# Gate and up of two feed forwards as seven block products instead of eight

## The chip, the cores and the metric

The kernel runs as one program on one core of one Trainium2 chip. The metric is device time in microseconds (us) of a whole run. The kernel before takes 2904.51 us, the median of three runs (2902.11 to 2906.32).

The engines' names in what follows are those of the profile: PE is TensorE (matmuls), PEld its weight load, DVE is VectorE, ACT is ScalarE, POOL is GpSimd, SP is SyncE, which issues most of the DMAs.

## The reference

The model is two transformer layers over 512 tokens and 256 context tokens, with 1024 features. A layer is: feed forward, attention, feed forward, each with an RMS norm, a learned shift and scale in front of it, and a gate on the result. What matters here, cut to the feed forwards:

```python
D_MODEL, SEQ, CTX_LEN, D_FF, DEPTH = 1024, 512, 256, 2816, 2

def _rmsnorm(x, w):
    y = x * lax.rsqrt(jnp.mean(x * x, axis=-1, keepdims=True) + EPS)
    return y * w

def _pre(h, gain, shift, scale):
    return _rmsnorm(h, gain) * (1.0 + scale) + shift

def _swiglu(h, w_gate, w_up, w_down):
    return (jax.nn.silu(h @ w_gate) * (h @ w_up)) @ w_down

for i in range(DEPTH):
    mx = (silu(c) @ ada_w[i] + ada_b[i]).reshape(B, 9, 1, D)      # the modulation, tokens
    mc = (silu(c_ctx) @ ada_w[i] + ada_b[i]).reshape(9, D)        # and context
    fx = _swiglu(_pre(hx, norm_w[i, 0], mx[:, 0], mx[:, 1]), ffn_w_gate[i, 0], ffn_w_up[i, 0], ffn_w_down[i, 0])
    hx = hx + 0.5 * mx[:, 2] * fx          # the same for hc with mc
    ...                                    # attention: i = 0 grouped, in windows; i = 1 differential
    fx = _swiglu(_pre(hx, norm_w[i, 2], mx[:, 6], mx[:, 7]), ffn_w_gate[i, 1], ffn_w_up[i, 1], ffn_w_down[i, 1])
    hx = hx + 0.5 * mx[:, 8] * fx          # the same for hc, but not in the last layer
return _rmsnorm(hx, final_norm_w)
```

All of it is in fp32. The four feed forwards are called first to fourth here: (layer 0, f 0), (0, 1), (1, 0), (1, 1). Attention stands between the first and the second and between the third and the fourth. The second and the third follow one another directly.

## The kernel before, in words

**Data.** Activations lie with features on the partitions: hT is [128, 8, 768], eight feature blocks, each with 256 context tokens and 512 tokens. An fp32 product is made from three matmuls in a faster format, which keeps only part of the mantissa: each operand is split into a high part (a cast) and a low part (what is left), and high x high, high x low and low x high are summed in PSUM. So every weight tile and every activation exists twice.

**Weights.** `weights` (its lines are 55 and 56 of the profile) reads 512 KB with a DMA that SP issues into w_raw (four buffers), ACT casts to w_hi (L55), and POOL subtracts to w_lo (L56); two buffers each.

**Input of a feed forward.** xh and xl, the scaled input in two parts, are made while the stage before writes its result: for each feature block d, as soon as the residual is in hT (`residual`, L311, DVE, reading PSUM), `x_block` squares it (ACT, L206), adds the squares into acc (POOL L208, the last block on DVE), and `x_parts` makes xh (ACT, L193) and xl (DVE, L194) for context and tokens. The normalization itself is linear, so its factor rstd is applied behind the projections. `norm` sums acc over partitions with a matmul against ones (PE, L239) and `rsqrt` makes rstd from it (ACT, and DVE L219 to L223).

**Blocks.** The 2816 hidden features are 22 blocks of 128. For a block, `project` (matmuls at L266) multiplies eight feature blocks x three parts x two column cuts of 384 tokens, for gate and again for up: 96 matmuls. Two extra columns carry the shift through the projection; they come out as the bias (DVE copy, L271). Then g = gate x rstd and u = up x rstd (DVE L304, PSUM input), silu on ACT, and the product (u + bias) x g in two parts, context and tokens (DVE, L961). ACT casts it to hh (L965), POOL subtracts to hl (L966).

**Down.** Blocks are taken in groups of 5, 5, 4, 4 and 4. A group's down projection (`gemm`, L68, L70, L72, per feature block d one PSUM tile with 256 and 512 columns) comes after the first block of the next group, the last group's at the end. There each d is followed by `x_block` of the next stage.

**Modulation.** The nine vectors of a layer are products of `ada_w` with two conditions. They are fill work: `ada_block` (L131) loads 512 KB and makes one or two products with a sum on DVE. 36 of these blocks fall into the second feed forward and 36 into the third.

**Order.** The engines' queues are in order. A scheduling pass of the framework decides, from the program's dependencies and a model of time, in which order each engine issues. Pools give buffers out again when their last reader is done. In PSUM, the feed forwards have four tiles "big" of two banks each.

## Time and profile before

| | |
|---|---|
| runs | 2904.51 us (2902.11 to 2906.32) |
| profiled execution | 2902.44 us, span 2900.6 us |
| mean granted clock of TensorE | 0.982 |
| PE busy | 2770.0 us, 95% of the span |
| DVE, POOL, ACT busy | 1555.9, 1311.2, 972.4 us |
| second feed forward | 986.8 to 1547.5 us |
| third feed forward | 1547.5 to about 2089 us |

How to read it: an engine's share of the span is an average over stages with different limits. PE's 95% says that it is the bound most of the time, not that the others have time at every place. In the rows that follow, a line is a group of instructions of one source line, engine and form, with its number, its mean duration and, in brackets, the idle time of its engine in front and what ended it. In views in order of time, the first number is the start in us from the beginning of the span, the second the duration. The stretches of a view of windows have, for every engine, the busy time and the number of instructions.

### The profile page before, as it was taken

Reading aid. Unit: us, or ns where it says so; the run is one execution under the profiler, and the core shown is the slowest. Engines: PE = TensorE matmul, PEld = TensorE weight load, DVE = VectorE, ACT = ScalarE, POOL = GpSimd, SP = SyncE. Lnnn points to the kernel's source line nnn. Section 1 sums busy time; section 2 is a strip of 40 time slices with the busy share of each in tenths; the row PEclk is TensorE's granted clock in tenths of the full one; section 3 lists DMA queues with packets and bytes.
Section 4 is the critical chain, followed back from the end, with each engine's and each line's share of the span. In section 5 each row is a group of like instructions: output and inputs, shape, how many; then the busy total and the mean of one; then the engine's idle time right before and its main releaser. Section 6 shows DMA issues by size and latency. Waiting matters only on the chain. (4 is left out here: it accounts for less than half of the span.)

```text
span 2900.6 us, 40961 instructions
## 1 busy us (share of the span) xinstructions
PE 2770.0 (95%) x16150; PEld 2593.4 (89%) x16150; DVE 1555.9 (54%) x2683; ACT 972.4 (34%) x1749; POOL 1311.2 (45%) x762
## 2 busy tenths in 40 slices
PE   5899999999989899999999999999989999999998
PEld 3899999989877799999998999999988887799998
DVE  7955555567887544444447333344467678522223
ACT  4322122145666421221224212221345555422223
POOL 4443343355443443333335433333465665555553
PEclk7999999999999999999999999999999999999999
DMA  6333333333242323233223232232232333233331
GB/s 240 121 112 108 125 105 118 124 115 100 82 144 81 99 78 112 76 106 117 74 90 106 75 118 84 91 120 88 85 98 74 90 89 114 83 92 100 102 105 44
DMA packets 113423, 296.38 MB, mean 102 GB/s; under 512 B 12880, under 2 KB 30928, under 8 KB 113232
## 3 DMA queue, kind: packets, MB, share of 16 engines
q1 hardware_dynamic: 112944, 293.66, 31.8%
q8 instruction: 128, 2.10, 0.3%
q14 instruction: 63, 0.52, 0.1%
q10 hardware_dynamic: 288, 0.10, 0.0%
HBM read 260.42 MB, written 15.20 MB: 95 GB/s over the span
## 5 line engine op out<-in xcount | busy, mean ns | idle before, releaser
L56 POOL TENSOR_TENSOR w_lo<-w_raw,w_hi 128x1024 fp32r<-128x1024 f32 (+2 forms) x377 | 802.1, 2128 | 1072.1 <-ACT w_hi L55 1055.6
L266 PE MATMUL big<-xh,w_hi 128*128 128x384 f32 (+3 forms) x2816 | 696.6, 328 | 38.7 <-DVE xh L831 19.5
L55 ACT CAST w_hi<-w_raw 128x1024 fp32r<-128x1024 f32 (+2 forms) x377 | 337.4, 895 | 1132.6 <-PE big L70 394.1
L266 PE MATMUL big<-xl,w_hi 128*128 128x384 f32 (+3 forms) x2816 | 693.6, 327 | 8.3 <-DVE xl L832 5.0
L266 PE MATMUL big<-xh,w_lo 128*128 128x384 f32 (+3 forms) x2816 | 693.6, 328 | 2.3 <-POOL w_lo L56 2.3
L266 PEld LDWEIGHTS big<-xh,w_hi 128*128 128x128 f32 x2816 | 502.5, 191 | 47.2 <-DVE xh L831 22.3
L266 PEld LDWEIGHTS big<-xl,w_hi 128*128 128x128 f32 x2816 | 500.3, 191 | 10.5 <-DVE xl L832 6.3
L266 PEld LDWEIGHTS big<-xh,w_lo 128*128 128x128 f32 x2816 | 497.8, 190 | 3.8 <-POOL w_lo L56 3.3
L131 DVE SCALAR_TENSOR_TENSOR ada_junk<-w_raw,s_bc 128x1024 f32<-128x1024 f32 x224 | 342.4, 1546 | 291.6 <-DMA w_raw<-ada_w 290.4
L271 DVE COPY bias<-big 128x2 f32<-128x2 f32 x176 | 27.7, 157 | 621.1 <-PE big L266 620.9
L68 PE MATMUL big<-hh,w_hi 128*128 128x512 f32 (+1 forms) x1200 | 327.6, 344 | 0.0
L70 PE MATMUL big<-hl,w_hi 128*128 128x512 f32 (+1 forms) x1200 | 327.3, 344 | 0.0
L72 PE MATMUL big<-hh,w_lo 128*128 128x512 f32 (+1 forms) x1200 | 326.8, 344 | 0.0
L311 DVE SCALAR_TENSOR_TENSOR hT<-big,mod,hT 128x512 f32<-128x512 f32 (+1 forms) x288 | 167.6, 618 | 176.7 <-PE big L72 176.4
L70 PEld LDWEIGHTS big<-hl,w_hi 128*128 128x128 f32 x1200 | 226.1, 188 | 29.5
L72 PEld LDWEIGHTS big<-hh,w_lo 128*128 128x128 f32 x1200 | 225.0, 188 | 28.6
L68 PEld LDWEIGHTS big<-hh,w_hi 128*128 128x128 f32 x1200 | 224.9, 188 | 27.2
L966 POOL TENSOR_TENSOR hl<-tb,hh 128x768 fp32r<-128x768 f32 (+1 forms) x88 | 152.3, 1730 | 183.2 <-ACT hh L965 181.9
L961 DVE SCALAR_TENSOR_TENSOR tb<-tb,bias,ta 128x512 f32<-128x512 f32 (+1 forms) x154 | 176.1, 1177 | 8.7 <-DVE tb L304 0.5
L285 PE MATMUL half<-xh,w_hi 128*128 128x384 f32 (+3 forms) x464 | 155.5, 335 | 20.6 <-DVE ta L297 18.8
L965 ACT CAST hh<-tb 128x768 fp32r<-128x768 f32 (+1 forms) x88 | 68.7, 781 | 276.5 <-DVE tb L961 276.5
L285 PE MATMUL half<-xl,w_hi 128*128 128x384 f32 (+3 forms) x464 | 153.8, 331 | 0.0
(215 smaller groups left out, 3677.6 us busy)
## 6 DMA issues: line engine op xcount, KB each, us to landing
w_raw<-ffn_gu SPq DMA_DIRECT2D x176, 512.0 KB, 3.3
w_raw<-ada_w SPq DMA_DIRECT2D x128, 512.0 KB, 3.3
w_raw<-ffn_d SPq DMA_DIRECT2D x96, 256.0 KB, 2.7
w_raw<-ffn_d SPq DMA_DIRECT2D x64, 320.0 KB, 2.9
w_raw<-diff_in SPq DMA_DIRECT2D x24, 512.0 KB, 3.2
ada_raw<-ada_w SPq DMA_DIRECT2D x16, 512.0 KB, 7.2
w_raw<-gqa_in SPq DMA_DIRECT2D x12, 512.0 KB, 3.5
og<-god SPq DMA_DIRECT2D x6, 768.0 KB, 6.5
```

The source lines that it names most:

```text
L55: nc.scalar.copy(out=hi[:, :cols], in_=raw[:, :cols])
L56: nc.gpsimd.tensor_tensor(out=lo[:, :cols], in0=raw[:, :cols], in1=hi[:, :cols].bitcast(F32), op=ALU.subtract)
L68: nc.tensor.matmul(o, wh, xh, start=(k == 0), stop=False)
L70: nc.tensor.matmul(o, wh, xl, start=False, stop=False)
L72: nc.tensor.matmul(o, wl, xh, start=False, stop=(k == n - 1))
L131: getattr(nc, engines[s]).scalar_tensor_tensor(out=junk, in0=raw, scalar=1.0, in1=self.sbc[:, s], op0=ALU.mult, op1=ALU.mult, accum_out=se ...
L266: mm(ps[:, c, :e - s], w[:, k], x[:, k, s:e], start=first, stop=last)
L285: mm(ps[:, :e - s], w_[:, k], x[:, k, s:e], start=(k == 0 and i == 0), stop=(k == ND - 1 and i == 2))
L311: self.nc.vector.scalar_tensor_tensor(out=h, in0=o, scalar=self.mv(l, s, c, d), in1=h, op0=ALU.mult, op1=ALU.add)
L961: nc.vector.scalar_tensor_tensor(out=u[:, tk], in0=u[:, tk], scalar=bu[:, s:s + 1], in1=g[:, tk], op0=ALU.add, op1=ALU.mult)
L965: nc.scalar.copy(out=hh[:, toks], in_=u[:, toks])
L966: nc.gpsimd.tensor_tensor(out=hl[:, toks], in0=u[:, toks], in1=hh[:, toks].bitcast(F32), op=ALU.subtract)
```

## The change

In the second and the third feed forward, a block's gate and up are one product of 2x2 blocks: the weight matrix has gate and up as its rows of blocks and the even and odd feature blocks as its columns; the input has the even and odd feature blocks as rows and the first and last 384 of the 768 tokens as columns. It is formed with seven products of blocks instead of eight, in the way of Strassen and Winograd: sums of weight blocks times sums of input blocks, added to the four results. A product is four pairs of feature blocks x three parts, 12 matmuls of 386 columns (384 and the two of the bias): 84 per block. The first and the fourth feed forward keep the old path.

With it comes:

- **Operands.** Instead of xh and xl there are seven operands for each pair of feature blocks, 28 slots in two tiles (opx, opy), each split into two parts. `operands`, called once per feature block where `x_block` was, makes them for every odd d: differences of scaled halves on DVE, casts on ACT, low parts on POOL or DVE.
- **Weight sums.** `up_open` loads the block's 2 x 512 KB and forms four sums of 512 columns (`total`, DVE); five halves of 512 and one of 1024 are split on ACT and POOL.
- **Results.** Products go to single PSUM banks (eight). Copies out of PSUM on ACT, additions from PSUM on DVE, and the scaling by rstd on DVE and POOL make g and u. Product 4 of a block, and with it all that follows (silu, product, hh, hl), is put into the next block (`up_end`).
- **Groups** of 4, 4, 4, 4, 3 and 3 blocks in these two stages; down projections with two feature blocks per weight load.
- **Buffers.** Weight tiles have one name and four buffers, in the new stages seven; the modulation's scratch is the tile `sq`; cos and sin are loaded inside the attention stages. The norm at the start is made in two halves.

```diff
 GROUPS = (5, 5, 4, 4, 4)
+GROUPS7 = (4, 4, 4, 4, 3, 3)
+KP = ND // 2
+HALF = T // 2
...
+    PROD = {1: (0, 0), 2: (1, 1), 3: (6, 2), 4: (2, 6), 5: (3, 3), 6: (4, 4), 7: (5, 5)}
...
+    def operands(self, l, n, d):
...
+        self.squares(d)
+        if d % 2 == 0:
+            return
...
+        def split(i, x, eng):
+            nc.scalar.copy(out=part(i, 0), in_=x)
+            eng.tensor_tensor(out=part(i, 1), in0=x, in1=part(i, 0).bitcast(F32), op=ALU.subtract)
+        def gained(i, h, e, cuts):
+            for s, tk in cuts:
...
+                nc.scalar.activation(out=hi, in_=h[:, tk], func=AF.Identity, scale=g(s, e))
+                stt(lo, h[:, tk], g(s, e), hi.bitcast(F32))
+        for s, tk in ((1, ctx), (0, mid)):
+            nc.vector.tensor_scalar(out=f0[:, tk], in0=h1[:, tk], scalar1=g(s, d - 1), scalar2=None, op0=ALU.mult)
+        split(0, f0, nc.gpsimd)
+        stt(t1, h1[:, end], g(0, d - 1), f0)
+        split(3, t1, nc.gpsimd)
+        stt(t2, h2[:, end], g(0, d), t1)
+        gained(1, h2, d, ((1, ctx), (0, mid)))
+        split(4, t2, nc.vector)
+        for s, tk in ((1, ctx), (0, mid)):
+            stt(t4[:, tk], h2[:, tk], g(s, d), t2[:, tk])
+        gained(2, h2, d, ((0, end),))
+        nc.vector.tensor_tensor(out=t3, in0=t2, in1=f0, op=ALU.subtract)
+        split(6, t4, nc.vector)
+        split(5, t3, nc.gpsimd)
...
+    def up_open(self, f, i):
...
+        def split(i, x):
+            t = self.wtile()
+            nc.scalar.copy(out=t[:, :512], in_=x)
+            nc.gpsimd.tensor_tensor(out=t[:, 512:], in0=x, in1=t[:, :512].bitcast(F32), op=ALU.subtract)
...
+        def total(x, y, op=ALU.subtract):
+            t = self.sums.tile([P, 512], F32, name="sum")
+            nc.vector.tensor_tensor(out=t, in0=x, in1=y, op=op)
+            return t
+        split(0, a11)
+        s1 = total(a21, a22, ALU.add)
+        split(3, s1)
+        hi, lo = self.wtile(), self.wtile()
+        nc.scalar.copy(out=hi, in_=raw[1])
+        nc.gpsimd.tensor_tensor(out=lo, in0=raw[1], in1=hi.bitcast(F32), op=ALU.subtract)
...
+        s2 = total(s1, a11)
+        split(4, s2)
+        split(6, total(a12, s2))
+        split(5, total(a11, a21))
...
+    def product(self, p, bank, ops, ks=range(KP), first=False):
...
+            for w, y, go, end in ((wh, xh, first and k == 0, False), (wh, xl, False, False),
+                                  (wl, xh, False, k == KP - 1)):
+                mm(o, w[:, k], y, start=go, stop=end, skip_group_check=not first)
...
+    def ffn7(self, which, l, f, side, after):
...
+        unit = self.up_open(which, 0)
+        for k in range(KP):
+            for p, c in ((1, 0), (5, 2), (2, 1)):
+                self.product(p, unit[1][c], unit[0], (k,), True)
+        for i in range(2):
+            ps = self.pbig.tile([P, 512], F32, name="bank")[:, :m]
+            tk = slice(i * m, i * m + m)
+            nc.tensor.matmul(ps, self.ones, self.acc[:, tk], start=True, stop=True)
+            self.rsqrt(self.rstd[:, tk], ps, 1.0 / D)
...
+        def up_block(i, hs):
+            ops, (ba, bb, bc) = self.up_open(which, i) if i else unit
...
+            if i:
+                self.product(1, ba, ops, first=True)
+            nc.scalar.copy(out=g[:, 0:w], in_=ba[:, :w])
+            if i:
+                self.product(5, bc, ops, first=True)
+            nc.scalar.copy(out=u[:, w:wide], in_=bc[:, B:w])
+            more()
+            if i:
+                self.product(2, bb, ops, first=True)
+            nc.vector.tensor_tensor(out=g[:, 0:w], in0=bb[:, :w], in1=g[:, 0:w], op=ALU.add)
+            self.product(6, ba, ops)
+            nc.scalar.copy(out=g[:, w:wide], in_=ba[:, B:w])
+            self.product(3, bc, ops)
+            nc.vector.tensor_tensor(out=g[:, w:wide], in0=bc[:, B:w], in1=g[:, w:wide], op=ALU.add)
+            nc.vector.tensor_tensor(out=g[:, B:wide], in0=g[:, B:wide], in1=self.rstd, op=ALU.mult)
+            if late:
+                up_end(*late.pop())
+            self.product(7, ba, ops)
+            nc.vector.tensor_tensor(out=u[:, w:wide], in0=ba[:, B:w], in1=u[:, w:wide], op=ALU.add)
+            nc.gpsimd.tensor_tensor(out=u[:, w:wide], in0=u[:, w:wide], in1=self.rstd[:, n2], op=ALU.mult)
+            late.append((ops, ba, g, u, hs))
```

How instructions move is seen at three places. The first is POOL in blocks of the second feed forward that have no down projection beside them. The rows are: line, operation, output <- inputs, shape; w_lo is a weight's low part, hl that of the block's result. Before, three operations are a block:

```order
L56 TENSOR_TENSOR w_lo_10425<-w_raw_10423,w_hi_10424 128x1024
L56 TENSOR_TENSOR w_lo_10488<-w_raw_10486,w_hi_10487 128x1024
L966 TENSOR_TENSOR hl_10419<-tb_10412,hh_10418 128x768
L56 TENSOR_TENSOR w_lo_10557<-w_raw_10555,w_hi_10556 128x1024
L56 TENSOR_TENSOR w_lo_10620<-w_raw_10618,w_hi_10619 128x1024
L966 TENSOR_TENSOR hl_10551<-tb_10544,hh_10550 128x768
```

Now, one block (L1052: a low half of 512 columns, one straight from w_raw and four from the sums; L1065: the low part of 1024 for the products 2 and 4; L1150: u's second half times rstd; L1124: hl):

```order
L1052 TENSOR_TENSOR w_9697<-w_raw_9693,w_9697 128x512
L1052 TENSOR_TENSOR w_9702<-sum_9700,w_9702 128x512
L1124 TENSOR_TENSOR hl_9673<-tb_9435,hh_9672 128x768
L1052 TENSOR_TENSOR w_9711<-sum_9709,w_9711 128x512
L1052 TENSOR_TENSOR w_9716<-sum_9714,w_9716 128x512
L1150 TENSOR_TENSOR tb_9580<-tb_9580,rstd_88 128x384
L1052 TENSOR_TENSOR w_9721<-sum_9719,w_9721 128x512
L1065 TENSOR_TENSOR w_9706<-w_raw_9694,w_9705 128x1024
```

Eight operations stand where three stood, and the largest of them, which is the third low part in the program's text, is the last of the block in the queue.

The second place is PE at the start of the second feed forward, where the norm's matmuls stand (acc against ones, L239 before and L1106 now). Before:

```order
L266 MATMUL big_9078<-xl_8697,w_hi_9080 128x384
L266 MATMUL big_9078<-xl_8697,w_hi_9080 128x386
L266 MATMUL big_9078<-xh_8696,w_lo_9081 128x384
L266 MATMUL big_9078<-xh_8696,w_lo_9081 128x386
L239 MATMUL big_9133<-acc_91,ones_80 128x384 x2
L266 MATMUL big_9166<-xh_8696,w_hi_9168 128x384
L266 MATMUL big_9166<-xh_8696,w_hi_9168 128x386
```

Now (bank_9113, 9114 and 9115 are block 0's results, bank_9255, 9257 and 9256 those of block 1):

```order
L1083 MATMUL bank_9114<-opy_8785,w_9128 128x386 x2
L1083 MATMUL bank_9114<-opy_8785,w_9129 128x386
L1083 MATMUL bank_9113<-opy_8785,w_9120 128x386 x2
L1083 MATMUL bank_9115<-opy_8785,w_9125 128x386 x2
L1106 MATMUL bank_9183<-acc_89,ones_80 128x384
L1106 MATMUL bank_9193<-acc_89,ones_80 128x384
L1083 MATMUL bank_9255<-opx_8784,w_9262 128x386 x9
L1083 MATMUL bank_9255<-opy_8785,w_9262 128x386 x3
L1083 MATMUL bank_9257<-opx_8784,w_9267 128x386 x6
L1083 MATMUL bank_9257<-opy_8785,w_9267 128x386 x6
L1083 MATMUL bank_9256<-opx_8784,w_9270 128x386 x2
L1083 MATMUL bank_9113<-opx_8784,w_9134 128x386 x6
```

In both, the norm stands behind the first products; before, these were gate and up of block 0, 96 matmuls, now they are three products of block 0, 36 matmuls, and two products of block 1 come ahead of the fourth of block 0 (bank_9113 again, its product 6).

The third place is DVE behind that norm (L219 to L223 before and L236 to L240 now make rstd; L131 before and L145 now are the modulation; L271 copies the bias). Before:

```order
L131 SCALAR_TENSOR_TENSOR ada_junk_9357,mod_89<-w_raw_9355,s_bc_9012 128x1024
L208 TENSOR_TENSOR acc_91<-sq_8998,acc_91 128x768
L131 SCALAR_TENSOR_TENSOR ada_junk_9359,mod_89<-w_raw_9355,s_bc_9012 128x1024
L271 COPY bias_9144<-big_9023 128x2
L271 COPY bias_9152<-big_9078 128x2
L219 TENSOR_SCALAR tb_9137<-big_9133 128x768
L221 TENSOR_TENSOR tb_9137<-tb_9137,ta_9136 128x768
L222 SCALAR_TENSOR_TENSOR tb_9137<-tb_9137,ta_9136 128x768
L223 SCALAR_TENSOR_TENSOR rstd_90<-tb_9137,ta_9136 128x768
```

Now, from the last sum of squares (L226) to the first half of rstd (L1057 is a sum of weights):

```order
L226 TENSOR_TENSOR acc_89<-sq_9060,acc_89 128x768
L145 SCALAR_TENSOR_TENSOR sq_9209,mod_87<-w_raw_9207,s_bc_9096 128x1024
L1057 TENSOR_TENSOR sum_9284<-w_raw_9258 128x512
L145 SCALAR_TENSOR_TENSOR sq_9211,mod_87<-w_raw_9207,s_bc_9096 128x1024
L236 TENSOR_SCALAR tb_9186<-bank_9183 128x384
L145 SCALAR_TENSOR_TENSOR sq_9319,mod_87<-w_raw_9317,s_bc_9096 128x1024
L238 TENSOR_TENSOR tb_9186<-tb_9186,ta_9185 128x384
L236 TENSOR_SCALAR tb_9196<-bank_9193 128x384
L145 SCALAR_TENSOR_TENSOR sq_9321,mod_87<-w_raw_9317,s_bc_9096 128x1024
L239 SCALAR_TENSOR_TENSOR tb_9186<-tb_9186,ta_9185 128x384
L238 TENSOR_TENSOR tb_9196<-tb_9196,ta_9195 128x384
L240 SCALAR_TENSOR_TENSOR rstd_88<-tb_9186,ta_9185 128x384
```

rstd's chain was three operations in a row behind its first; now two half chains and four products of the modulation stand between one another, and ta_9185 is the buffer that g of block 0 takes next.

More of the change, by code (lines that the diff above doesn't have):

```diff
@@ L51, in weights @@
         raw = self.rawp.tile([P, 1024], F32, name="w_raw")
[L52 to L53 removed]
+        hi = self.wtile()
+        lo = self.wtile()
         nc.sync.dma_start(raw[:, :cols], src)
```

217 lines of the change are left out of this document (183 added, 34 removed).

## The prediction, made before the changed kernel was run

> **What bounds the kernel now.** I read the page first, then the stretches of the two feed forwards that change, then the order of time inside one block, and last the seams between the stages.
>
> ```profile
> span 2900.6 us, 40961 instructions
> PE 2770.0 (95%) x16150; PEld 2593.4 (89%) x16150; DVE 1555.9 (54%) x2683; ACT 972.4 (34%) x1749; POOL 1311.2 (45%) x762
> ```
>
> ```profile
> 1151.10:1168.10 17.00, 17.00 (x98) 17.00 (x98) 7.46 (x11) 4.12 (x6) 7.18 (x3) 1.00 0.28 93
> 986.80:1547.50 560.70, 560.70 (x3172) 537.56 (x3173) 265.76 (x379) 134.20 (x176) 222.82 (x112) 1.00 0.29 93
> 1547.50:2089.00 541.50, 535.67 (x3027) 513.92 (x3026) 214.48 (x307) 119.77 (x155) 202.21 (x101) 0.99 0.29 95
> ```
>
> Columns of the second fence: stretch, length, then busy time of PE, weight load, DVE, ACT, POOL, the granted clock, DMA. The second feed forward is 986.8 to 1547.5 and the third 1547.5 to about 2089; PE is busy in all of the one and all but 6 us of the other. So TensorE alone sets the time there, and matmuls taken away are worth their full time as long as nobody else becomes late. Who could is seen inside one block without a down projection (VectorE's rows, then POOL's):
>
> ```profile
> 1151.13 0.16 DVE L271 COPY bias<-big 128x2 f32<-128x2 f32 x1 [6.91 <-PE big L266]
> 1151.21 0.95 DVE L304 TENSOR_TENSOR tb<-big,rstd 128x768 f32<-128x768 f32 x1
> 1152.27 3.01 DVE L961 SCALAR_TENSOR_TENSOR tb<-tb,bias,ta 128x256 f32<-128x256 f32 x2
> 1159.89 1.23 DVE L131 SCALAR_TENSOR_TENSOR ada_junk<-w_raw,s_bc 128x1024 f32<-128x1024 f32 x1
> 1168.08 0.16 DVE L271 COPY bias<-big 128x2 f32<-128x2 f32 x1 [6.02 <-PE big L266]
> ```
>
> ```profile
> 1151.95 2.39 POOL L56 TENSOR_TENSOR w_lo<-w_raw,w_hi 128x1024 fp32r<-128x1024 f32 x1 [6.05 <-ACT w_hi L55]
> 1156.23 1.84 POOL L966 TENSOR_TENSOR hl<-tb,hh 128x768 fp32r<-128x768 f32 x1 [1.89 <-ACT hh L965]
> 1160.42 2.95 POOL L56 TENSOR_TENSOR w_lo<-w_raw,w_hi 128x1024 fp32r<-128x1024 f32 x1 [2.36 <-ACT w_hi L55]
> ```
>
> From one bias copy of "up" to the next (1151.13 to 1168.08) a block takes 16.95 us for 96 matmuls. The two L961 together take 3.01 us while POOL works; and POOL's 2.39 us become 2.95 when a VectorE product is under way. The medians and extremes say which operations do this (min/median/max in ns):
>
> ```profile
> L961 DVE SCALAR_TENSOR_TENSOR tb<-tb,bias,ta x88: 472/740/2358, 1019.2 to 2083.2; 128x256 f32<-128x256 f32 x44, 128x512 f32<-128x512 f32 x44
> L304 DVE TENSOR_TENSOR ta<-big,rstd x44: 946/948/953, 1015.4 to 2072.8; 128x768 f32<-128x768 f32 x44
> L324 POOL TENSOR_TENSOR tb<-tb,sin x16: 1265/1278/1977, 2139.9 to 2418.2; 128x512 f32<-128x512 f32 x16
> L324 DVE TENSOR_TENSOR tb<-tb,sin x10: 676/693/2060, 648.4 to 826.1; 128x512 f32<-128x512 f32 x10
> L208 DVE TENSOR_TENSOR acc<-sq,acc x2: 953/956/959, 992.6 to 1561.0; 128x768 f32<-128x768 f32 x2
> L460 DVE TENSOR_SCALAR p<-p,st x24: 335/522/877, 679.8 to 934.7; 128x512 f32<-128x512 f32 x8, 128x640 f32<-128x640 f32 x8, 128x256 f32<-128x256 f32 x8
> ```
>
> An operation with one input in PSUM (L304) never varies, though POOL works beside it at 1151.95. One with both inputs in SBUF (L961) waits until POOL's instruction is over: 2.36 instead of 0.47. So POOL and VectorE take turns on one thing, and their times add. That sum, not either engine's share, is what the change must be held against.
>
> **The change, part by part.** *Matmuls.* A block has 84 of 386 columns for 96 of 384 and 386, so 16.95 x 84/96 = 14.83 us (0.177 a matmul); 44 blocks save 44 x 2.12 = **-93 us**. The down projection keeps its count.
>
> *Turns per block (blocks with no down beside them).* POOL now makes five halves of 512 (1.28 each, 6.4), one of 1024 (2.39), hl of 768 (1.84) and a product of 384 columns, 1.0 by the step from 1.28 at 512 to 1.84 at 768. Sum 11.6. VectorE's operations with both inputs in SBUF: four totals of 512 at 0.69 (2.8), the scaling of g over 768 (0.96), L1119's two, 0.47 and 0.74 (1.2). The modulation adds per block two of 1.23 in the second feed forward (36 blocks of weights for two streams) and mostly one in the third (36, of which 4 for two). Sums: 11.6 + 5.0 + 2.5 = **19.1** and 17.9 us, against 14.83 of PE. Each change of hands overlaps a little: L961's pair would take 0.47 + 0.74 alone and ends at 1155.28, so it began at 1154.07, 0.27 before POOL's end; POOL's 2.95 ends at 1163.37, so its 2.39 began 0.14 before L131's end at 1161.12. With some 12 changes a block at 0.17, and 0.5 idle where POOL's product waits for VectorE to add from PSUM, the turns need 17.6 and 16.4: 2.8 and 1.6 over PE.
>
> The first excess is hidden. The lo half for product 2 may be written after product 5 of its block (in the built program it takes that product's buffer), and PE reaches it after product 4, 2 matmuls, product 6 and 8 matmuls: 34 x 0.177 = 6.0 us, less 2.39 of POOL leaves 3.6. Between downs 5, 4, 4, 4, 3 and 2 blocks follow each other. Stall per run is blocks x excess - 3.6: second feed forward 10.4 + 3 x 7.6 + 4.8 + 2.0 = 40, third 4.4 + 3 x 2.8 + 1.2 = 14. I take **+50**, as part of the first run falls into the start counted below. Bounds: 0 if all is absorbed, and without any overlap (4.3 and 3.1 over) 73 + 46 = 119.
>
> [...]
>
> *The seams.* Here the operands are made, on the path into the first products.
>
> ```profile
> 978.08 0.52 PE L520 MATMUL half<-og,w_lo 128*128 128x256 f32 x2
> 986.80 0.98 PE L266 MATMUL big<-xh,w_hi 128*128 128x384 f32 x2 [8.20 <-DVE hT L311]
> 1557.89 0.62 PE L266 MATMUL big<-xl,w_hi 128*128 128x384 f32 x2 [3.27 <-DVE xl L194]
> 1558.35 0.76 PE L266 MATMUL big<-xh,w_lo 128*128 128x384 f32 x2
> 1561.64 0.69 PE L266 MATMUL big<-xh,w_hi 128*128 128x384 f32 x1 [2.53 <-ACT xh L193]
> ```
>
> ```profile
> 956.70 1.18 DVE L311 SCALAR_TENSOR_TENSOR hT<-half,mod,hT 128x256 f32<-128x256 f32 x2 [0.58 <-PE half L520]
> ```
>
> ```profile
> 1218.72 0.52 PE L68 MATMUL big<-hh,w_hi 128*128 128x256 f32 x2
> ...
> 1225.00 0.51 PE L68 MATMUL big<-hh,w_hi 128*128 128x256 f32 x2
> ```
>
> ```profile
> 1530.51 1.84 POOL L208 TENSOR_TENSOR acc<-sq,acc 128x768 f32<-128x768 f32 x1 [0.91 <-ACT sq L206]
> 1532.30 1.75 POOL L56 TENSOR_TENSOR w_lo<-w_raw,w_hi 128x512 fp32r<-128x512 f32 x1
> 1534.97 1.85 POOL L208 TENSOR_TENSOR acc<-sq,acc 128x768 f32<-128x768 f32 x1 [0.92 <-ACT sq L206]
> ```
>
> PE idles 8.2 us at the first seam (attention to second feed forward), 5.8 at the second (to the third), and there the last down already runs by turns: 4.46 us from sum to sum. Per pair of feature blocks VectorE will have, with inputs in SBUF: three of 384 columns with a scalar (0.61 each, between 0.47 at 256 and 0.74 at 512), two cut into 256 + 128 (0.83, same step), three plain of 384 (0.55, by the step from 0.69 to 0.96), and two scalings (0.59, from L460's 0.34 at 256): 5.7. Four pairs make 22.9; the last sum 0.96 and totals of 0.69, seven at the first seam and four at the second, bring 28.7 and 26.6. POOL has, up to that last sum, six sums of 1.84, twelve or eleven splits of 1.0, and weight halves of 13.6 or 8.8: 36.6 and 30.8. PE cannot pass that sum: line 1106's matmuls with acc stand in its queue ahead of the second block. Together 65.3 and 57.4 us, less 25 POOL operations x 2 changes x 0.17 = 8.5. Beside it PE has, at the first seam, from the first pair's sum (957.9) to 978.6, 20.7 us; at the second, the last four feature blocks, 36 pairs of 256 and 512 columns at 0.349 (18 pairs lie between the two L68 rows), 12.6; and at each the 36 first products, 6.3. Idle 29.8 and 30.0, net of today's 8.2 and 5.8 **+46**. Bounds: 8 if POOL alone counted, 63 without overlap at the changes.
>
> *Start of each feed forward.*
>
> ```profile
> 1006.10 1.45 PE L239 MATMUL big<-acc,ones 128*128 128x384 f32 x4
> 1013.38 0.96 DVE L223 SCALAR_TENSOR_TENSOR rstd<-tb,ta 128x768 f32<-128x768 f32 x1
> ```
>
> Today 8.2 us lie between acc's matmuls and the end of rstd, and PE has two "big" tiles to go on with. Now the first half's chain holds the ta buffer that g of block 0 needs, with four modulation products (4.9 us) queued among its steps on VectorE; product 6 of block 0 waits for g's copy, and PE has 26 matmuls (4.6 us) until then. 8.2 + 4.9 - 4.6 is 8.5 each; I take **+12** for both, bounds 0 and 20. The wait for hh of the last block ahead of the last down, which fewer blocks cover, and the seam to the attention, with 9 pairs of matmuls a feature block for 12, I take as **+6**, bounds 0 and 10. DMA moves the same bytes at a share of 0.29; ACT gains casts, but is busy 134 of 560 us: nothing for both while each stays under a block's 14.8 us.
>
> Sum: -93 + 50 + 46 + 12 + 6 = **+21 us**, on the profiled execution's 2902.4 (span 2900.6 and 1.8 around it): 2923. The median of the runs is 2904.5, 2.1 higher, so **2926**.
>
> **Rivals.** *The turns are absorbed (faster).* If buffers and the down projections, in which POOL and VectorE have time left, let the work run ahead, the stall in runs falls to 5 and the seams hide half their work: -93 + 5 + 23 + 6 + 3 = -56, 2848. For it: POOL is busy only 222 of 560 us today, and every weight half is wanted microseconds after it may be made. Against it: the queues are in order, and the shared sum of a block is above PE's. It decides when a block's turns need under 14.83 + 3.6/4 = 15.7 us.
>
> *The clock drops in the runs (much slower).* After a wait of 3.27 us the pairs at 1558.35 take 0.76 instead of 0.52, and after 8.2 us this stands in the profile:
>
> ```profile
> 986.80:992.00 5.20, 5.20 (x17) 5.20 (x18) 4.36 (x3) 1.54 (x3) 3.34 (x2) 0.52 0.31 101
> ```
>
> A clock of 0.52 for 5.2 us loses 2.6. If the stalls come as one wait above some 3 us, twice in each of ten full runs, that is +52: 2978. Spread over several waits, they cost nothing more. The Trainium skill ("TensorE: Matmul & The Clock Gate", "Part 1: The HAM clock gate") puts the limit at one idle window of about 3.4 us; the row shows that 3.27 was enough here.
>
> *A wash.* Costs of about 93 instead of 114: 2904.
>
> **How the numbers follow.** Forecast 0.47 (own range 2911 to 2955), absorbed 0.32, clock 0.13, wash 0.08. A difference below 0.2%, 5.8 us, can hardly be told from none: faster 0.32, same 0.08, slower 0.60. The bounds together span 2904.5 - 85 to + 119; 8 in 10 is 2842 to 2980, which leaves out the lower part of the absorbed case and the upper part of the clock's.
>
> **What would show it.** Right: blocks in runs 16 to 18 us apart, with PE waiting for POOL's halves at line 1083; L1119 and the totals (L1057) at means well over 0.7; some 30 us of PE idle ahead of line 1106, twice; PE's busy time down by about 90. Wrong: blocks 15 us apart with VectorE still blocked (absorbed), or seams under 20 us. If PE's matmuls of 386 columns were slower than 0.177 us apart, the gain itself would be off.

## The result and the profile after

The changed kernel takes 2968.91 us (2966.26 to 2969.41, four runs) against 2903.31 us (2901.91 to 2906.32) for the kernel before in the same comparison: 1.0223 times as long, 95% interval 1.0205 to 1.0240, or 65.6 us more. The forecast was 2926 us, 21 us more. The side was right, and the time lies inside the range of 8 in 10 (2842 to 2980). It lies 14 us above the forecast's own range (2911 to 2955): the size was a third of what came. Its profiled execution took 2969.22 us with a span of 2967.2 us.

The head of the page, and the stretches of the second and third feed forward (stretch, length, busy PE, weight load, DVE, ACT, POOL, granted clock, DMA):

```profile
span 2967.2 us, 40899 instructions
...
PE 2717.9 (92%) x15622; PEld 2519.2 (85%) x15622; DVE 1917.3 (65%) x3067; ACT 1107.9 (37%) x2063; POOL 1591.3 (54%) x974
```

```profile
985.70:1606.00 620.30, 537.84 (x2909) 501.22 (x2908) 478.75 (x592) 210.78 (x347) 386.82 (x225) 0.95 0.28 89
1606.00:2175.00 569.00, 528.62 (x2908) 497.36 (x2908) 386.10 (x489) 196.98 (x324) 344.08 (x207) 0.97 0.31 95
```

Where PE was busy all the time but 6 us, it is now idle 82 and 40 us; its clock is 0.95 and 0.97 instead of 1.00 and 0.99. VectorE is busy 479 us in the second feed forward instead of 266, POOL 387 instead of 223; time in which an operation is blocked counts as busy.

What PE waits for inside the runs of the second feed forward (who waits for whom; us in total, times, longest):

```profile
PE bank L1083 <- DVE tb L1149: 17.5, 6, 5.2
PE bank L78 <- DVE hT L328: 8.9, 3, 5.0
PE bank L78 <- ACT hh L1123: 3.4, 4, 1.9
PE bank L1083 <- POOL w L1065: 2.7, 1, 2.7
```

One such wait in order of time, first VectorE, then POOL, then PE (start, duration):

```profile
1482.93 2.09 DVE L145 SCALAR_TENSOR_TENSOR sq<-w_raw,s_bc 128x1024 f32<-128x1024 f32 x1
...
1485.06 2.19 DVE L145 SCALAR_TENSOR_TENSOR sq<-w_raw,s_bc 128x1024 f32<-128x1024 f32 x1
...
1487.18 2.85 DVE L1057 TENSOR_TENSOR sum<-w_raw,sum 128x512 f32<-128x512 f32 x1
1489.96 0.55 DVE L1144 TENSOR_TENSOR ta<-bank,ta 128x384 f32<-128x384 f32 x1
1490.54 0.96 DVE L1145 TENSOR_TENSOR ta<-ta,rstd 128x768 f32<-128x768 f32 x1
1491.41 0.68 DVE L1057 TENSOR_TENSOR sum<-w_raw 128x512 f32<-128x512 f32 x1
1492.02 0.55 DVE L1149 TENSOR_TENSOR tb<-bank,tb 128x384 f32<-128x384 f32 x1
```

```profile
1481.94 2.00 POOL L1124 TENSOR_TENSOR hl<-tb,hh 128x768 fp32r<-128x768 f32 x1
1483.90 2.27 POOL L1052 TENSOR_TENSOR w<-sum,w 128x512 fp32r<-128x512 f32 x1
1486.13 3.36 POOL L1065 TENSOR_TENSOR w<-w_raw,w 128x1024 fp32r<-128x1024 f32 x1
```

```profile
1488.09 0.51 PE L1083 MATMUL bank<-opx,w 128*128 128x386 f32 x2
1492.62 0.69 PE L1083 MATMUL bank<-opx,w 128*128 128x386 f32 x1 [4.03 <-DVE tb L1149]
```

From 1482 to 1490 the two engines take turns. Two modulation products take 2.09 and 2.19 us (1.23 at the median), a weight sum 2.85 (0.69 alone); POOL's low parts of 512 and 1024 columns take 2.27 and 3.36 (1.28 and 2.39 alone). VectorE reaches L1144 at 1489.96, and behind it L1149, which reads the bank that PE's next product adds to. PE has stood since 1488.6. What is waited for is an operation of VectorE that itself takes 0.55 us and is never blocked (537 to 559 ns over all 44; one of its inputs is in PSUM); it stands in a queue behind operations that wait for their turn.

To compare kernels by stage, PE's time beyond its matmuls is worked out from the trace of each kernel's one profiled execution: the distance from each matmul's start to the next, less 0.1755, 0.1764, 0.1204 and 0.2304 us for 384, 386, 256 and 512 columns (the distances where nothing disturbs). What is over 0.6 us counts as waiting, the rest as slowness. "Seam 2" runs from 940 us to 3 us behind the second feed forward's first norm matmul, "start" covers the next 27 us, "seam 3" goes from 60 us ahead of the third's norm to 3 behind, "seam d" from 8 us ahead of the differential attention to 30 us into it; "runs" are what lies between a start and the next seam. Each entry is waiting + slowness, in us:

| kernel | seam 2 | start 2 | runs 2 | seam 3 | start 3 | runs 3 | seam d |
|---|---|---|---|---|---|---|---|
| before | 10.8+4.9 | 0.0+0.1 | 0.0+0.3 | 6.3+2.8 | 0.0+0.1 | 0.0+0.4 | 5.6+3.1 |
| the change | 34.8+6.0 | 3.0+1.9 | 40.8+14.7 | 34.6+3.9 | 2.7+1.7 | 23.4+6.9 | 12.2+4.7 |
| no modulation | 34.4+5.6 | 2.7+1.3 | 8.2+2.7 | 34.0+5.2 | 0.7+1.9 | 10.0+3.0 | 13.7+5.2 |
| modulation, no loads | 34.0+5.3 | 5.0+4.1 | 46.0+18.6 | 33.8+4.1 | 4.6+3.2 | 25.9+12.9 | 11.2+4.4 |
| low parts on VectorE | 26.0+7.4 | 7.4+3.6 | 12.2+4.9 | 19.8+4.9 | 13.4+5.5 | 8.7+0.7 | 13.2+5.0 |
| last group of four | 33.1+8.5 | 2.3+2.4 | 39.1+16.7 | 28.1+7.1 | 2.8+2.0 | 27.9+13.2 | 7.7+2.2 |
| seam on VectorE | 21.3+9.7 | 12.1+4.3 | 39.7+15.5 | 23.7+4.3 | 11.6+3.0 | 25.5+9.0 | 12.1+2.9 |
| norm later | 30.6+7.7 | 4.6+2.9 | 40.8+16.8 | 27.1+6.3 | 4.1+4.3 | 22.0+8.7 | 14.4+4.4 |
| all moves | 17.9+6.6 | 7.1+3.3 | 9.3+2.7 | 17.0+3.9 | 2.8+4.1 | 12.0+2.4 | 4.7+2.2 |
| six banks | 33.0+7.4 | 2.4+2.2 | 42.1+19.1 | 32.1+4.5 | 3.3+1.7 | 22.2+8.8 | 3.9+3.6 |
| six banks, condition in PSUM | 33.0+7.2 | 2.1+2.6 | 35.0+11.5 | 31.0+6.0 | 2.8+2.3 | 14.3+8.3 | 5.2+3.3 |

The first two rows account for the result. The matmuls need 91 us less. Against that stand 25.1 + 29.4 at the two seams, 4.8 + 4.3 in the starts, 55.2 + 29.9 in the runs, 8.2 at the differential attention, and 1.3 elsewhere: +67, of 66.6 in the spans.

### The profile page after: what moved, and what is told of

It is laid out like the page before. It is cut to its first block, busy times and chain, and to the rows that moved or that the text cites. A ratio compares the mean times of both kernels' runs of the same rounds, so it can differ in the third digit from the quotient of the medians.

```text
span 2967.2 us, 40899 instructions
## 1 busy us (share of the span) xinstructions
PE 2717.9 (92%) x15622; PEld 2519.2 (85%) x15622; DVE 1917.3 (65%) x3067; ACT 1107.9 (37%) x2063; POOL 1591.3 (54%) x974
## 5 line engine op out<-in xcount | busy, mean ns | idle before, releaser
L66 POOL TENSOR_TENSOR w<-w_raw,w 128x1024 fp32r<-128x1024 f32 (+3 forms) x257 | 570.5, 2222 | 538.2 <-ACT w L65 480.0
L1083 PE MATMUL bank<-opx,w 128*128 128x386 f32 x2112 | 446.1, 349 | 73.9 <-DVE tb L1149 28.1
L145 DVE SCALAR_TENSOR_TENSOR sq<-w_raw,s_bc 128x1024 f32<-128x1024 f32 x224 | 355.5, 1587 | 215.9 <-DMA w_raw<-ada_w 214.1
L1083 PEld LDWEIGHTS bank<-opx,w 128*128 128x128 f32 x2112 | 388.0, 195 | 88.9 <-DVE tb L1149 31.4
L1083 PE MATMUL bank<-opy,w 128*128 128x386 f32 x1584 | 339.3, 345 | 11.3 <-DVE opy L1005 5.3
L1052 POOL TENSOR_TENSOR w<-sum,w 128x512 fp32r<-128x512 f32 x176 | 270.4, 1546 | 104.7 <-ACT w L1051 104.5
L1083 PEld LDWEIGHTS bank<-opy,w 128*128 128x128 f32 x1584 | 290.9, 193 | 13.1 <-ACT opy L1009 6.0
L283 PE MATMUL big<-xh,w 128*128 128x384 f32 (+1 forms) x1312 | 289.1, 341 | 0.8 <-POOL w L66 0.8
L283 PE MATMUL big<-opx,w 128*128 128x256 f32 x2112 | 256.2, 284 | 2.7 <-DVE hT L328 2.4
L78 PE MATMUL bank<-hh,w 128*128 128x256 f32 (+1 forms) x704 | 186.3, 341 | 20.0 <-DVE hT L328 11.0
L302 PE MATMUL half<-opx,w 128*128 128x384 f32 (+3 forms) x1008 | 180.1, 327 | 16.9 <-DVE ta L314 16.7
L1051 ACT CAST w<-sum 128x512 fp32r<-128x512 f32 x176 | 106.1, 619 | 213.8 <-PE bank L80 80.4
L82 PE MATMUL bank<-hh,w 128*128 128x256 f32 (+1 forms) x704 | 179.0, 337 | 0.5 <-POOL w L66 0.5
L1065 POOL TENSOR_TENSOR w<-w_raw,w 128x1024 fp32r<-128x1024 f32 x44 | 112.2, 2549 | 80.0 <-ACT w L1064 36.4
```

The lines of the kernel that those rows point to most:

```text
L66: nc.gpsimd.tensor_tensor(out=lo[:, :cols], in0=raw[:, :cols], in1=hi[:, :cols].bitcast(F32), op=ALU.subtract)
L78: nc.tensor.matmul(o, wh, xh, start=(k == 0), stop=False)
L82: nc.tensor.matmul(o, wl, xh, start=False, stop=(k == n - 1))
L145: getattr(nc, engines[s]).scalar_tensor_tensor(out=junk, in0=raw, scalar=1.0, in1=self.sbc[:, s], op0=ALU.mult, op1=ALU.mult, accum_out=se ...
L283: mm(ps[:, c, :e - s], w[:, k], x[:, k, s:e], start=first, stop=last)
L302: mm(ps[:, :e - s], w_[:, k], x[:, k, s:e], start=(k == 0 and i == 0), stop=(k == ND - 1 and i == 2))
```

## The experiments

Four theories of the waits in the runs and at the seams stand against each other. A: VectorE and POOL take turns, and the sum of their turns is late. B: VectorE's queue stands behind the modulation's loads. C: POOL's low parts alone are late. D: VectorE alone has too much work, wherever its operands lie. Where no range of several executions is given, a time below is that of one execution; four executions of the change lie within 3.2 us.

**Only the buffer edits, on the kernel before.** (Here "theory A" is that of the buffers.)

```diff
-        self.wp = self.sb("weights", 2)
+        self.wp = self.sb("weights", 4)
...
-            junk = pool.tile([P, D], F32, name="ada_junk")
+            junk = self.tq.tile([P, D], F32, name="sq")
...
+        self.load_rope(lp)
```

> The kernel before with only the change's buffer edits: one weight name with four buffers, the modulation's scratch in the tile sq, cos and sin loaded inside the attention stages. No block products. In the changed kernel the first feed forward, whose code is the same, ends 7.6 us later than before (636.5 against 628.9 us), and from the third feed forward's end to the fourth's first matmul it takes 398.5 us against 388.0. Theory A: the first feed forward's 7.6 us come from these buffer edits, which move the order of the loads at the start, and the 10.5 us from the shorter last group of three blocks; then this kernel takes 5 to 10 us more than before and its attention stages are as before within 2 us. Rival: both come from engines that are late because of the block products; then this kernel is within 2 us of before. Second rival: both come from the buffer edits; then it takes 15 to 20 us more.

It took 2902.41 us, the kernel before 2904.29 beside it: no difference. But the stages moved. The attention behind the first feed forward begins 6.8 us later, nearly as much as with the whole change (its first matmul, in order of time, of before, of the change and of this kernel):

```profile
628.94 0.34 PE L285 MATMUL s<-xh,w_hi 128*128 128x384 f32 x1
```

```profile
636.54 0.34 PE L302 MATMUL s<-xh,w 128*128 128x384 f32 x1
```

```profile
635.71 0.34 PE L288 MATMUL s<-xh,w 128*128 128x384 f32 x1
```

In the order of SP's queue this kernel has one modulation block and one weight load earlier among the loads of the start than the kernel before; in the three kernels below that put the modulation's scratch back into its own tile the order is the old one, and the attention begins at 629.5 to 630.2 us. So the first half of this theory A holds: an edit for the second feed forward costs 7 us in the first. Its forecast of the whole, 5 to 10 us more, does not: this kernel wins 5.7 us of idle at the second feed forward's first products (2.5 in place of 8.2); why was not tested. The differential attention takes 390.2 us here, 388.0 before and 398.5 in the change, so most of its 10.5 us do not come from the buffers. One wait of the first seam does go with them: that for the DMA `og<-god` in the output projection is 2.3 us before, 5.4 here and 6.0 in the change.

**No modulation in the two feed forwards.**

```diff
-        self.ffn7(0, 0, 1, [(1, b) for b in range(36)], lambda d: self.operands(1, 0, d))
+        self.ffn7(0, 0, 1, [], lambda d: self.operands(1, 0, d))
```

> The changed kernel without the modulation of layer 1 in the second and third feed forward: neither its loads nor its products (the vectors are zero instead, so layer 1 adds nothing; all other work is there). Theory A (VectorE and POOL take turns, and their sum is what the blocks wait for): 2.5 us of turns a block are gone in the second and 1.2 to 1.4 in the third feed forward, 36 x 2 x 1.23 + 40 x 1.23 = 138 us of VectorE in all; PE's waits inside the runs (about 39 and 25 us now, and some 20 us at a lower clock) fall below a third; 2895 to 2925 us. Theory B (the wait is for the modulation's loads, behind which VectorE's queue stands): the same here, and told apart by the next kernel. Theory C (POOL's low parts alone are late): VectorE's load does not matter and it stays above 2950 us.

This kernel leaves out the loads and the products; the modulation of layer 1 is zero in it. 2906.80 us, as A and B have it. Waiting in the runs falls from 64.2 to 18.2 us and slowness from 21.6 to 5.7. POOL's work is unchanged, so C falls: less work on VectorE is enough. The waits at the seams stay (34.4 and 34.0 us).

**The modulation without its loads.**

```diff
-        raw = self.rawp.tile([P, 1024], F32, name="w_raw")
-        (q or nc.sync).dma_start(raw, self.a["ada_w"][l, b])
+        raw = None
+        if l == 0:
+            raw = self.rawp.tile([P, 1024], F32, name="w_raw")
+            (q or nc.sync).dma_start(raw, self.a["ada_w"][l, b])
...
-                out=junk, in0=raw, scalar=1.0, in1=self.sbc[:, s], op0=ALU.mult, op1=ALU.mult,
+                out=junk, in0=self.sbc[:, 1 - s] if raw is None else raw, scalar=1.0, in1=self.sbc[:, s], ...
```

> The changed kernel with the modulation products of layer 1, but without their loads: each product takes the other condition's row, which is in SBUF already, in place of the weights (so the modulation of layer 1 has other values). VectorE's work is the same, its waits for these loads and their share of the four raw buffers are gone. Theory A (turns): nearly as slow as the changed kernel, 2945 to 2970 us, since the sum of the turns is unchanged. Theory B (VectorE's queue stands behind loads that are late, 35 and 37 us of its idle time in the two feed forwards): about as fast as the kernel without modulation, 2895 to 2925 us.

The products take other inputs here, so the modulation of layer 1 has other values. 2986.62 us: B falls. It is even 18 us slower than the change, which no theory expected (A's range ended at 2970). In the changed kernel 42 of the 112 products lie beside a down projection, where VectorE and POOL have time; here 23 do. Without the loads to wait for, more of them come inside the runs. That fits A, but was only counted in the two traces, not tested by itself.

**The low parts of a block on VectorE.** In three lines `nc.gpsimd` becomes `nc.vector`:

```diff
-            nc.gpsimd.tensor_tensor(out=t[:, 512:], in0=x, in1=t[:, :512].bitcast(F32), op=ALU.subtract)
+            nc.vector.tensor_tensor(out=t[:, 512:], in0=x, in1=t[:, :512].bitcast(F32), op=ALU.subtract)
...
-        nc.gpsimd.tensor_tensor(out=lo, in0=raw[1], in1=hi.bitcast(F32), op=ALU.subtract)
+        nc.vector.tensor_tensor(out=lo, in0=raw[1], in1=hi.bitcast(F32), op=ALU.subtract)
...
-            nc.gpsimd.tensor_tensor(out=hl, in0=u[:, B:wide], in1=hh.bitcast(F32), op=ALU.subtract)
+            nc.vector.tensor_tensor(out=hl, in0=u[:, B:wide], in1=hh.bitcast(F32), op=ALU.subtract)
```

> The changed kernel with the low parts of a block's weights and of its result (lines 1052, 1065 and 1124) on VectorE instead of POOL; all work is done, POOL keeps u's scaling, the down projections' low parts and the sums of squares. Theory A (turns): what counts is the sum over both engines, and VectorE does the same subtraction in about half the time (512 columns 0.69 against 1.28, 768 in 0.96 against 1.84): five halves, one of 1024 and one of 768 fall from 10.6 to 5.7 us a block, the sum from 19.1 to 14.2 us (17.9 to 13.0 in the third feed forward), VectorE with its 2.4 us from PSUM to 15.6 and 14.4. Against PE's 14.83 most of the waits inside runs go: 2910 to 2945 us. Theory D (each engine for itself, VectorE is the one that is late): VectorE's work per block rises from 9.9 to 15.6 us and all 44 blocks become later, more than 2985 us.

2912.09 us, inside A's range and 57 less than the change, with all work done. VectorE got 308 instructions more and is hardly busier, because its operations wait less: a low half of 512 columns takes 732 ns there, and L1119's larger form has a mean of 1095 ns, in the change 1671. First this kernel's page, to be held against the change's above, then two groups of its VectorE, then the same group of the change:

```profile
PE 2708.6 (93%) x15622; PEld 2511.7 (86%) x15622; DVE 1954.7 (67%) x3375; ACT 1112.3 (38%) x2063; POOL 1086.4 (37%) x666
```

```profile
L1052 DVE TENSOR_TENSOR w<-sum,w 128x512 fp32r<-128x512 f32 x171 | 123.1, 732 | 22.0 <-ACT w L1051 21.8
...
L1119 DVE SCALAR_TENSOR_TENSOR tb<-tb,bias,ta 128x512 f32<-128x512 f32 x44 | 48.2, 1095 | 0.0
```

```profile
L1119 DVE SCALAR_TENSOR_TENSOR tb<-tb,bias,ta 128x512 f32<-128x512 f32 x44 | 73.5, 1671 | 0.0
```

And the wait for L1149 is gone (this kernel's waits of PE in the runs of the second feed forward):

```profile
PE bank L78 <- DVE hT L328: 4.8, 3, 4.2
PE bank L78 <- ACT hh L1123: 3.5, 2, 2.0
...
PE bank L1083 <- DVE tb L1149: 0.8, 1, 0.8
```

With D this would have been over 2985 us. VectorE was late because of what POOL did beside it, not because of its own amount of work alone. It shows in the blocks too. Where no down projection lies between two L1149, they are 17.6 and 16.9 us apart in the mean of the change's second and third feed forward, and 14.8 and 14.7 here; 84 matmuls at full clock take 14.8.

**Three changes at the seams, one at a time, on the changed kernel.**

```diff
-GROUPS7 = (4, 4, 4, 4, 3, 3)
+GROUPS7 = (3, 3, 4, 4, 4, 4)
```

> The changed kernel with the groups in the order 3, 3, 4, 4, 4, 4 in place of 4, 4, 4, 4, 3, 3 (same buffers, same work). The last down projection has 12 in place of 9 pairs of matmuls for each feature block, 4.2 instead of 3.1 us, beside which the next stage's input is made. Theory A (the seams are set by the turns of VectorE and POOL from the first residual on, whatever PE does beside them): 8 x 1.05 = 8.4 us less idle at the seam to the third feed forward and as much at the one to the differential attention, which goes back from 398.5 to about 390 us; 2949 to 2955 us. Rival: the longer attention start comes from the loads of cos and sin inside the stage; then it stays at 397 to 400 us and the whole at 2957 to 2963.

2975.49 us, slower than both forecasts (2949 to 2955, 2957 to 2963). Seam 3 and the one to the differential attention lose 3.3 and 7.0 us, less than the 8.4 expected of each, and the runs of the third feed forward become 10.8 longer; why was not tested. The attention's stretch goes back from 398.5 to 388.6 us; but with six banks and the old groups (below) it takes 387.4 too, so that the short last group isn't shown to be its cause.

```diff
-            eng = nc.vector if d == ND - 1 else nc.gpsimd
+            eng = nc.vector if d == ND - 1 else eng or nc.gpsimd
...
-        self.squares(d)
+        self.squares(d, eng=nc.vector)
...
-        split(0, f0, nc.gpsimd)
+        split(0, f0, nc.vector)
```

(and the same for the splits 3 and 5)

> The changed kernel with the seams' POOL work on VectorE: the six sums of squares a seam (1.84 us on POOL, 0.96 on VectorE) and three low parts of 384 columns for each pair of feature blocks (1.0 against 0.55). Theory A (turns): the seam's sum falls by 6 x 0.88 + 12 x 0.45 = 10.7 us and by the handovers that go, PE's idle ahead of the two norms by 8 to 12 us each; 2945 to 2953 us. Theory D (VectorE alone is late at the seam): its work there grows from 28.7 to 41 us, and the idle grows by up to 12 us each: over 2975 us.

2970.75 us, between the forecasts of A (2945 to 2953) and D (over 2975). The seams shrink by 9.8 and 10.5 us, as A has it. But the starts grow by 11.5 and 10.2: PE's wait at the norm's matmuls is gone and comes back behind them. At the first seam it is 8.5 us for ACT's copy of block 0 (L1133), whose buffer the norm's chain holds:

```profile
L1083 PE MATMUL bank<-opx,w 128*128 128x386 f32 x58 | 18.2, 467 | 19.4 <-ACT ta L1133 8.5 <-ACT w L1051 7.7 <-POOL w L1065 2.3
...
L1106 PE MATMUL bank<-acc,ones 128*128 128x384 f32 x4 | 2.9, 888 | 0.0
```

```diff
             self.product(7, ba, ops)
             nc.vector.tensor_tensor(out=u[:, w:wide], in0=ba[:, B:w], in1=u[:, w:wide], op=ALU.add)
+            if not i:
+                norm()
+                nc.vector.tensor_tensor(out=g[:, B:wide], in0=g[:, B:wide], in1=self.rstd, op=ALU.mult)
```

> The changed kernel with the norm's two matmuls behind block 0's seventh product in the program (72 or 84 matmuls of block 0 ahead of them in place of 36), and g's scaling behind the norm. In the changed kernel PE waits 6.3 and 10.2 us there for the last sum of squares. Theory A: the matmuls that now stand behind the norm fill this wait, as their operands are made before the sum or with it; 10 to 16 us less, 2953 to 2959 us. Rival: the operands of the products 6, 3 and 7 are as late as the sum (they come out of the same turns), and PE waits for them instead: 2965 to 2970 us.

2972.97 us, 3 above the rival's range and 14 above A's: at the first seam the wait at the norm falls from 6.3 to 1.2 us, and that for ACT's casts of weights (L1051) rises from 12.6 to 15.8. None of the three is worth anything alone.

**All moves together.** The edits of the last four, and

```diff
-            junk = self.tq.tile([P, D], F32, name="sq")
+            junk = pool.tile([P, D], F32, name="ada_junk") if l == 0 else self.tq.tile([P, D], F32, name="sq")
```

> All four together: a block's low parts on VectorE, the seams' POOL work on VectorE, groups 3, 3, 4, 4, 4, 4, the norm behind block 0's products; and the modulation's scratch in the first feed forward in its old place, which gives the start its old order of loads (6.8 us later with the buffer edits alone). All of the work is done. Theory A (turns): from 2912 us of the low parts alone, less 7 for the start, 10 to 16 for the groups, 10 to 20 for the seams, 5 to 15 for the norm: 2860 to 2885 us, faster than before. Theory D (VectorE as the bound): with still more on VectorE it is slower than the low parts alone, over 2912 us.

2877.96 us (2875.89 to 2880.34, four runs) against 2901.28 of before: ratio 0.9924, interval 0.9908 to 0.9941. That is inside A's range and beats both kernels, by 23 and by about 91 us. What brought nothing alone does here: seams and starts together stand at 62.7 us, at 88.6 in the change, 88.0 with the low parts alone and 90.0 with the seams' work alone. That the turns no longer make something else late is the reading that fits; the moves were not taken out one by one, except for the norm's place below. POOL is down to 1027 us:

```profile
span 2874.1 us, 40693 instructions
...
PE 2697.5 (94%) x15622; PEld 2506.6 (87%) x15622; DVE 1936.9 (67%) x3411; ACT 1113.0 (39%) x2063; POOL 1027.4 (36%) x630
```

**One operand in PSUM.** First the control, the changed kernel with six banks:

```diff
-        self.pbig = self.ps("pffn7", 8)
+        self.pbig = self.ps("pffn7", 6)
```

> The changed kernel with six PSUM banks for the products in place of eight, as a control for the next one. A block holds three banks and one of the block before, and a down projection two, so both theories expect little: within 15 us of the changed kernel, rather slower.

2961.58 us, 7 less than the change rather than more, and within the 15 expected; 8.3 us of waiting less stand at the seam to the differential attention. Then, with six banks, the first condition's row in PSUM:

```diff
+        pcond = self.ps("pcond", 1)
+        self.cond = pcond.tile([P, D], F32, name="cond")
+        nc.scalar.copy(out=self.cond, in_=self.sbc[:, 0])
...
-                out=junk, in0=raw, scalar=1.0, in1=self.sbc[:, s], op0=ALU.mult, op1=ALU.mult,
+                out=junk, in0=raw, scalar=1.0, in1=self.sbc[:, s] if s or self.cond is None else self.cond, ...
```

> The changed kernel with the first condition's row (4 KB a partition) copied to two PSUM banks at the start of each of the two feed forwards; the 72 modulation products of that condition read it there, the 40 of the other stay as they are. Nothing else differs from the control with six banks. Theory A (an operation with one input in PSUM takes no part in the turns): the products of this condition take about 1.23 us each whatever POOL does (1.6 us in the mean now), and 72 x 1.23 = 89 us leave the turns: PE's waits inside the runs (64 us, and 21 at a lower clock) fall by half or more, 30 to 50 us less than the control. Theory D (VectorE is late because of the sum of its own work, wherever the inputs lie): the products take as long on VectorE's queue, and it is within 12 us of the control.

2943.42 us, 18 less than the control. The same operation on the same queue, by where its second input lies (duration in ns, min/median/max):

```profile
L145 DVE SCALAR_TENSOR_TENSOR sq<-w_raw,s_bc x152: 1207/1226/3466, 42.3 to 1659.2; 128x1024 f32<-128x1024 f32 x152
...
L145 DVE SCALAR_TENSOR_TENSOR sq<-w_raw,cond x72: 1202/1220/1223, 1021.3 to 2081.9; 128x1024 f32<-128x1024 f32 x72
```

All 72 products with one input in PSUM take 1202 to 1223 ns; those with both in SBUF up to 3466. So the operation does what A says of it. The kernel does not: waiting and slowness in the runs fall from 92.2 to 69.1 us, a quarter where A gave half, and the 18 us lie between A's 30 to 50 and D's 12, nearer to D's. The other operations stay blocked about as long as in the control (L1119's larger form 1768 ns in the mean against 1746, POOL's halves from the sums 1485 against 1567); why the turns that are left cost so much was not tested.

**The norm's place once more.** All moves, but the norm as in the change:

```diff
+        for i in range(2):
+            ps = self.pbig.tile([P, 512], F32, name="bank")[:, :m]
+            tk = slice(i * m, i * m + m)
+            nc.tensor.matmul(ps, self.ones, self.acc[:, tk], start=True, stop=True)
+            self.rsqrt(self.rstd[:, tk], ps, 1.0 / D)
```

> All moves together (2878 us) but with the norm where the changed kernel has it. The norm behind block 0 cost 6 us on the changed kernel alone. Theory A: with the sums on VectorE the sum of squares is early enough and the norm's place costs or brings under 6 us: 2872 to 2884. Rival: the start's waits (12 and 10 us idle behind the norm when the seam's work alone was moved, 7 and 3 with all moves) come back, 2885 to 2895 us.

2886.65 us, the rival: 9 us come back, and waiting in the starts is 9.9 and 11.8 us in place of 7.1 and 2.8. So the later norm is worth something only once the sum is early.

**All moves and the condition in PSUM.**

> All moves together, and the first condition in PSUM with six banks. What is left to win are the waits in the runs, 9 and 12 us idle and 5 at a lower clock. Theory A: half of it and some of the starts, 2860 to 2872 us, if six banks cost nothing. Theory D: no gain, or slower by what six banks cost: 2876 to 2890 us.

2875.55 us (2870.81 to 2877.09, four runs), ratio 0.9906 to before, interval 0.9890 to 0.9923. This is the fastest median, but not to be told from the moves without it (2875.89 to 2880.34). It lies just below D's range (2876 to 2890) and above A's (2860 to 2872): once the low parts have left POOL, the condition in PSUM brings nothing that can be told.

## Why the prediction was right or wrong

| term of the sum | predicted | measured |
|---|---|---|
| matmuls | -93 | -91 |
| turns in the runs | +50 | +85 (waiting 64, slower clock 21) |
| seams | +46 | +54.5 |
| starts | +12 | +9 |
| last group, seam to the attention | +6 | +8 |
| everything else | 0 | +1 |

**Right.** What bounds: the matmuls taken away are worth what they were counted at. That POOL and VectorE take turns, that their sum is the price of the change, and that it outweighs the gain: the low parts on VectorE show it for the kernel, the condition in PSUM for the single operation. The blocks' distance, 17.6 and 16.9 us in the mean, is what the prediction's turns gave (17.6 and 16.4), though part of it is slower clock. The seams' idle, predicted at 30 each, is 34.8 and 34.6. The signs named ahead: L1119 has means of 1671 and 1355 ns, and the wait at line 1106 is there, but with 6.3 and 10.2 us it is only part of the seam; the rest is waited for at the first products. The change's first seam, then its second (idle time and what ended it behind the second bar):

```profile
L1083 PE MATMUL bank<-opx,w 128*128 128x386 f32 x25 | 8.2, 461 | 12.6 <-ACT w L1051 12.6
L1083 PE MATMUL bank<-opy,w 128*128 128x386 f32 x12 | 4.3, 466 | 6.6 <-DVE opy L1005 5.3 <-ACT opy L1009 1.3
L1106 PE MATMUL bank<-acc,ones 128*128 128x384 f32 x4 | 2.9, 887 | 6.3 <-DVE acc L226 6.3
```

```profile
L1083 PE MATMUL bank<-opx,w 128*128 128x386 f32 x26 | 7.8, 457 | 15.2 <-DVE hT L328 15.2
L1083 PE MATMUL bank<-opy,w 128*128 128x386 f32 x12 | 4.2, 452 | 4.7 <-ACT opy L1009 3.8 <-POOL opy L1010 0.9
L1106 PE MATMUL bank<-acc,ones 128*128 128x384 f32 x4 | 2.9, 888 | 10.2 <-DVE acc L226 10.2
```

PE's busy time fell by 52 us and not by the 90 named: the matmuls that are left took longer in the trace, in part at the lower clock.

**Wrong: the size, at the step of the turns in the runs.** Two things are missing there.

First, the clock. The prediction kept it out of the sum ("spread over several waits, they cost nothing more") and made it a rival that begins with one wait above some 3 us. The waits did come spread, 33 in the runs, six of them over 3 us and five of 2 to 3, and the clock fell behind nine of these eleven. Behind the wait of 4.03 us shown above, and behind one of 3.60 us (length, busy times, clock):

```profile
1492.62:1497.50 4.88, 4.88 (x15) 4.88 (x16) 0.61 (x3) 2.78 (x6) 4.17 (x4) 0.50 0.56 188
1405.50:1410.50 5.00, 5.00 (x19) 5.00 (x20) 1.10 (x3) 3.27 (x6) 2.89 (x3) 0.66 0.08 32
```

In runs and starts together slowness is 25.2 us, 0.9 before: 24 us, over half of what the forecast lacks. So the step that failed first is a term put at nothing: what a wait of 2 to 5 us costs behind its end. This is read from the traces; no run was made for the clock alone. It goes with the waits, though: 5.7 us are left in the runs without modulation, 5.6 with the low parts on VectorE.

Second, the waiting itself: 64 us where 50 were taken, and 54 was the sum of the two feed forwards (40 and 14; measured 41 and 23). The model was right that a run has an excess per block, but it looked at the wrong instruction. It expected PE at POOL's low half for product 2 (L1065); there PE waits 2.7 and 1.5 us in the two feed forwards. The largest part, 17.5 and 10.6 us, is for VectorE's L1149, behind which product 4 stands. VectorE's queue holds the modulation's products, the sums and L1119 ahead of it, and these wait for POOL. So the cover of 3.6 us, worked out for product 2, belongs to a wait that hardly came, and that the second feed forward's 40 came out as 41 is luck in part.

The seams are 8.5 us over. Of the first, 6.0 us are the wait for a DMA in the attention's output projection, where before there were 2.3; that was not foreseen, and 5.4 are there with the buffer edits alone.

**The other stages** came out at +1 by cancelling: the first feed forward costs 7.6 us more, through an edit that the prediction passed over because its code lies elsewhere, and the first attention has some 6 us less of waiting and slowness outside the seam.

**The rivals.** The turns were not absorbed: 64 us against the 5 of that case. A wash would have needed 93 us of cost, it is 158. The clock's case was priced at +52 on top, twenty falls of 2.6 us; it gives 24, which is some twelve falls at the 2 us that one costs here. The measured time lies nearer to that rival's 2978 us, which had a chance of 0.13, than to the forecast's 2926; the rival had the missing mechanism, but its condition, one long wait twice in each of ten runs, did not come about.

## What to carry to other kernels

Two engines that take turns on SBUF are one engine for planning: add up the operations of POOL and of VectorE with two inputs in SBUF, over a block, and hold the sum against PE's time for that block, before looking at either's share. If the sum is too large, put the work on the faster of the two, even if that is the one being waited for (VectorE took 0.73 us where POOL takes 1.28, and the kernel won 57 us). Bringing one input from PSUM takes an operation out of the turns, but here gave less than its sum promised. And where PE begins to wait in pieces, add about 2 us of low clock to each piece of 3 us or more, and about half of that to one of 2 to 3; these prices are from the kernels of this study.

## What was not expected of the hardware

**The clock can fall behind waits well under 3 us.** From all traces of this study, the waits of PE in the second and third feed forward that have no other wait in the 12 us ahead or the 7 us behind, and how many of them are followed by over 1 us of slowness in those 7 us:

```
wait, us      waits   followed by slowness   mean loss, us
0.6 to 1.5      71            0                  0.2
1.5 to 2.0      19            4                  0.5
2.0 to 2.5      16            8                  0.9
2.5 to 3.0      10            8                  1.4
3.0 to 8.0      43           43                  2.0
```

So it comes behind some waits between 1.5 and 3 us and behind all of those above that were seen, and costs 1.4 to 2.9 us when it happens. What decides between 1.5 and 3 us is open. The Trainium skill ("TensorE: Matmul & The Clock Gate", "Part 1: The HAM clock gate") has a free-running window of about 3.4 us. A window that runs by itself agrees with the same wait being enough at one time and not at another; that half of the waits of 2.0 to 2.5 us are enough does not agree with one whole idle window of that length.

**By the profile's times a turn is handed over before it ends.** L145 at 1485.06 ends at 1487.25; alone it takes 1.23 us, so it began at 1486.02, and POOL's L1052 ended at 1486.17: 0.15 us of overlap, as in the trace of before (0.14 to 0.27). No run tells whether the turn ends early or POOL's end is recorded late. The Trainium skill ("SBUF — State Buffer", "SBUF: two separate sides") says of a VectorE operation with two inputs in SBUF and a GpSimd operation that reads SBUF that whichever starts first has the shared ports for its whole instruction, and the other fully blocks; the rows show that, but for this overlap.

**An unchanged stage moves by 7 us** when another tile's place changes which loads the scheduling pass puts first: the first attention begins at 635.7 us with the buffer edits alone, at 628.9 without them.
